# Hybrid decoder block: two heads' q and k as one pair of seven products, and the order of the gate pairs

## The chip, the cores and the metric

The kernel runs on one core of one Trainium2 chip. The metric is the device time of one execution in microseconds. A profile is one execution taken by the hardware profiler; its span runs from the first to the last instruction of the program. In the profile PE is TensorE (matmuls, with PEld its weight loads), DVE is VectorE, ACT is ScalarE, POOL is GpSimd and SP is SyncE, which here only issues transfers.

## The reference

One decoder block on 512 tokens of width 1024, in float32:

```python
hn = rmsnorm(x, g_mix)
(xa, ba, ca, za, q, k, v, o, zb, ig, fg, ga, gb) = split(hn @ w_in)        # w_in: 1024 x 14344
ya = (ba * causal_short_conv(ca * xa, conv_w, conv_b) * silu(za)) @ w_a_out
hb = mlstm_chunkwise(q, k, v, ig + b_i, fg + b_f)                           # 4 heads, dk 256, dv 512
yb = (sigmoid(o) * rmsnorm(hb, g_head) * silu(zb)) @ w_b_out
x = x + (sigmoid(ga) * ya + sigmoid(gb) * yb) @ w_o
x = x + sigmoid(rmsnorm(x, g_ple) @ w_ple_gate) * (p @ w_ple)
return rmsnorm(x, g_final)
```

q and k are 1024 columns each (256 for a head), v, o and zb 2048 each (512 for a head), ga and gb 1024 each. The mLSTM of a head needs the scores q k^T under a mask with running gate terms, and multiplies them by v. The kernel takes each head over all 512 tokens at once.

## The kernel before

**Matmuls in three parts.** Each float32 operand is cut into a high part (rounded to the matmul's format, `hi`) and a low part (the rest, `lo`). `mm3` (L203) issues three matmuls: hi x hi, hi x lo, lo x hi. The cut of a weight takes ScalarE for `whi` (L152) and VectorE for `wlo` (L153); each weight operand of 512 x 512 is cut in two halves of 128 x 1024.

**Plain blocks and pairs.** A plain block (`block_fm`, L267) multiplies all 1024 rows of hn by 512 columns of weights: two operands, 2 x 4 x 4 x 3 = 96 matmuls of 512 columns. A pair (`strassen`, L293) does 1024 columns with seven products instead of eight (Strassen's scheme in Winograd's form): the weights' blocks b11, b21, b12, b22 are added up in the raw buffers, and the left side's combinations of hn are kept cut in `hs` (L255). A pair with tokens on the output's partitions takes 7 x 24 = 168 matmuls of 512 columns; with `fm=True` (features on the partitions, 256 tokens of a half along the columns) it takes 7 x 48 = 336 of 256 columns. The convolution's four pairs are of the second kind, all others in this kernel of the first. The outputs of a pair need 6 sums `c` on VectorE (L325) and 8 copies out of PSUM on ScalarE (`snap`, L321); `c` has 3 buffers.

**Weights.** `chunks` lists the transfers and `operands` (L69 to L120) the order in which the products use them. Four raw buffers (`wraw`) rotate; SyncE's queue loads a chunk as soon as a buffer is free. The sums of a pair are made by adding transfers on GpSimd's queue (L159): they read the other block from memory again and add it to a raw buffer, after that buffer's present content has been cut. Where a pair's third sum has an engine (`third`, `dve`), VectorE makes that sum instead (L157).

**Order.** All engines but SyncE execute in the order in which the code emits. After each quarter or half of a product the code calls `step` (L195): a `tick` cuts one half of the next operand and moves every pending generator (`active`) one `yield` on. So a pair has 14 ticks, a plain block 8. An operand is cut one product ahead of its use, and a transfer that adds to a buffer has two products' time.

**Stages.** PLE product and transposes of x into `hn_hi`, `hn_lo` (`turn_x`, L501; GpSimd adds them back to `hnf`, L506); Q0, the plain block of q and k of head 0, kept in memory (`keep_qk`, L621) after its ScalarE copy (L623); between its second half's two middle banks the 16 gate matmuls `psg` (L708), whose small rows then go through `gate_rows` (L637: scans, logarithms, and 14 small transposes `ptc`, L685 and L687); then the pair GB. Beside GB run `gate_rows` and `left` (L611), which makes `hs` from the four combinations at L606 to L609. Then for each head h: q and k (head 0 loads its raw ones back into `qk_raw`; others run a plain block, Q1 to Q3), the pair VO (v and o, with the head's `scores` in its ticks), the weighted sums (L862), and for even heads the pair ZB for this head and the next. `finish` (L908) transposes a head's result and stores it (`yt_d`) in the ticks of the next stage. After head 3 comes the pair GA, then the convolution's four pairs, the products with w_a_out, w_b_out, w_o and w_ple_gate, and the last norm.

So the order of the large stages is Q0, GB, VO0, ZB0, Q1, VO1, Q2, VO2, ZB2, Q3, VO3, GA, convolution.

Of the kernel before, what the change touches and what calls it, by code (L numbers as in the profile page):

```python
# [14 lines left out]
P = 128  # L15
# [21 lines left out]
def hybrid_block(ctx, tc, x, p, g_mix, w_in, conv_w, conv_b, w_a_out, b_gates, g_head,  # L37
# [206 lines left out]
    qk_d = dram.tile([P, 4, S], F32, name="qk_d")  # L244
# [118 lines left out]
    def sink_conv(c, u, v, ya, ct):  # L363
# [13 lines left out]
        def put(src, h):  # L377
            to = [t[:, c:c + 2, h * H2:(h + 1) * H2] for t in ya]
# [122 lines left out]
    def turn_x(k):  # L501
# [4 lines left out]
        pool.tensor_tensor(hnf[:, k, :], hn_hi[:, k, :].bitcast(F32), hn_lo[:, k, :].bitcast(F32), ALU.add)  # L506
# [95 lines left out]
    a11, a12 = (hnf[:, c * HC:(c + 1) * HC, :H2] for c in range(2))  # L602
    a21, a22 = (hnf[:, c * HC:(c + 1) * HC, H2:] for c in range(2))
    hsf = [sp.tile([P, HC, H2], F32, name=f"hsf{i}", tag=f"hsf{i}", align_bytes=256) for i in range(2)]

    dve.tensor_tensor(hsf[0], a22, a21, ALU.subtract)  # L606
    dve.tensor_tensor(hsf[1], hsf[0], a11, ALU.add)
    dve.tensor_tensor(a12, hsf[1], a12, ALU.subtract)
    dve.tensor_tensor(a21, a11, a21, ALU.subtract)  # L609

    def left():  # L611
        for i, src, scale in ((0, hsf[0], 1.0), (3, a12, 1.0), (1, hsf[1], -1.0), (2, a21, 1.0)):
            act.activation(hs[i][0], src, AF.Copy, scale=scale)
            yield
            dve.scalar_tensor_tensor(hs[i][1], src, scale, hs[i][0].bitcast(F32), ALU.mult, ALU.subtract)
            yield
# [4 lines left out]
    def keep_qk(m, ps):  # L621
        u = temp("eevv"[m], "qk_s")
        act.activation(u, ps, AF.Copy)  # L623
        nc.gpsimd.dma_start(qk_d[:, m, :], u)
        yield
# [11 lines left out]
    def gate_rows():  # L637
# [14 lines left out]
        yield  # L652
# [39 lines left out]
        for _ in range(4):  # L692
            yield
        act.activation(enm.rearrange("p t h -> p (t h)"), colsb[:, 40:], AF.Exp)

    colsb = const.tile([P, 56], F32, name="colsb")
    enm = const.tile([P, NT, NH], F32, name="enm")

    w = next_operand()
    for m in range(4):  # L700
# [3 lines left out]
        step(keep_qk(m, pss[m]))  # L704
        if m == 1:
            psg = ps_x.tile([P, S], F32, name="psg", tag="x")
            for k in range(KT):
                pe.matmul(psg, lhsT=wg[:, k, :], rhs=hn_hi[:, k, :], start=k == 0, stop=False)  # L708
                pe.matmul(psg, lhsT=wg[:, k, :], rhs=hn_lo[:, k, :], start=False, stop=k == KT - 1)
            active.append(gate_rows())  # L710
# [10 lines left out]
    strassen(hn_lhs, sink_gate(0))  # L721
# [27 lines left out]
    def scores(h, qk, pr, pp, done, raw):  # L749

        if raw is not None:
            yield
            yield
            for m in range(4):
                cut(qk[0][:, m, :], qk[1][:, m, :], raw[:, m, :])
                if m == 1:
# [8 lines left out]
                          cmask.unsqueeze(1).broadcast_to([P, NT, P]), ALU.add)  # L765
        sc, e = {}, {}
# [26 lines left out]
    def head(h):  # L793
        qk, vv = [], []

        def cut_qk(m, ps):
            if not qk:
                both = hp.tile([P, 2, 4, S], F32R, name="qk", tag="qk", align_bytes=256)
                qk.extend(both[:, i] for i in range(2))
            if m is None:  # L800
                return
            cut(qk[0][:, m, :], qk[1][:, m, :], ps)
            yield

        raw = None
        if h == 0:
            next(cut_qk(None, None), None)
# [438 lines left out]
```

## Time and profile before

| | |
|---|---|
| median of 3 runs | 871.14 us (869.73 to 873.0) |
| the profiled execution's own time | 871.68 us |
| its span | 869.7 us |
| granted TensorE clock, mean | 0.996 |
| transfers | 169.65 MB, mean 195 GB/s |

Busy times of engines are unions of their instructions' spans. A matmul's recorded duration is longer than the distance to the next one, since matmuls overlap; what one costs is read from the distance of starts. A wait is put down to the instruction that released it. The chain lists, backwards from the last instruction, what each step waited for.

### The profile page before, as it was taken

The page shows a single profiled execution, that of the slowest core. Times are in us where ns is not written, and L with a number is a line of the kernel's source. Part 1 is how long each engine was busy: PE and PEld are TensorE (multiplying, and loading weights), DVE is VectorE, ACT ScalarE, POOL GpSimd, SP SyncE. Part 2 cuts the span into 40 slices and gives each one's busy share as a digit, 9 for nine tenths or more (in the row PEclk, how much of TensorE's full clock was granted, in tenths as well). Part 3 has the DMA queues.
Part 4 walks back from the last instruction along what each step waited for, and adds up shares of the span by engine and source line. Part 5 has one row for each costly group of instructions (what it writes and reads, how often), then busy time and mean ns, then how long its engine had stood idle before and what let it go on. Part 6 is the DMA issues. An engine that isn't in the chain of part 4 may idle for free.

```text
span 869.7 us, 11799 instructions
## 1 busy us (share of the span) xinstructions
PE 852.3 (98%) x4507; PEld 732.3 (84%) x4507; DVE 599.8 (69%) x774; ACT 468.4 (54%) x674; POOL 255.8 (29%) x246
## 2 busy tenths in 40 slices
PE   7999999999999999999999999999999999999995
PEld 6877888888888888888888999999998888788885
DVE  4769676774674666755785588898986777864465
ACT  5575676555563755547656555545453256534342
POOL 3742422322333132331331424333410224030031
PEclk9999999999999999999999999999999999999999
DMA  8799996968855887867869989899898588994002
GB/s 289 262 210 220 275 221 127 223 233 193 177 163 145 191 176 158 238 193 158 236 122 269 230 192 163 202 181 181 181 326 309 97 194 211 272 329 157 1 1 97
DMA packets 100728, 169.65 MB, mean 195 GB/s; under 512 B 6272, under 2 KB 44224, under 8 KB 99392
## 3 DMA queue, kind: packets, MB, share of 16 engines
q0 software_dynamic: 39312, 76.03, 45.1%
q1 hardware_dynamic: 60208, 90.78, 31.5%
q10 hardware_dynamic: 1152, 2.10, 0.7%
q8 instruction: 35, 0.57, 0.3%
q14 instruction: 21, 0.17, 0.1%
HBM read 153.16 MB, written 15.73 MB: 194 GB/s over the span
## 4 chain that ended last, share of the span: by engine, by line
PE 80%; DMA 6%; issue 4%; DVE 4%; ACT 2%; POOL 2%; POOLq 0%; SPq 0%; DVEq 0%; ACTq 0%
PE mm L206 24%; PE mm L207 24%; PE mm L205 24%; DMA wraw<-in_w_in 3%; DMA wraw<-in_w_b_out 2%; DVE wlo L153 2%; PE pv L205 1%; ACT whi L152 1%; PE pv L206 1%; PE pv L207 1%; POOL wraw L159 1%; PE pty L744 1%; DMA sg_d<-c 1%; DMA pin<-in_p 0%; PE sc L207 0%
## 5 line engine op out<-in xcount | busy, mean ns | idle before, releaser
L153 DVE TENSOR_TENSOR wlo<-wraw,whi 128x1024 fp32r<-128x1024 f32 x234 | 299.1, 1281 | 127.3 <-ACT whi L152 127.0
L152 ACT ACTIVATE whi<-wraw 128x1024 fp32r<-128x1024 f32 x236 | 247.0, 1054 | 105.2 <-PE mm L207 44.7
L159 POOL DMA_DIRECT2D wraw<-in_w_in x110 | 136.0, 1402 | 289.1 <-DVE wlo L153 218.5
L205 PE MATMUL mm<-hn_hi,whi 128*128 128x256 f32 (+1 forms) x320 | 105.1, 328 | 0.0
L207 PE MATMUL mm<-hn_hi,wlo 128*128 128x256 f32 (+1 forms) x320 | 104.4, 326 | 0.2 <-POOL wlo L153 0.2
L206 PE MATMUL mm<-hn_lo,whi 128*128 128x256 f32 (+1 forms) x320 | 104.2, 326 | 0.0
L206 PE MATMUL mm<-wlo,hs 128*128 128x512 f32 x256 | 100.7, 393 | 1.1 <-DVE wlo L153 1.0
L205 PE MATMUL mm<-whi,hs 128*128 128x512 f32 x256 | 101.0, 394 | 0.3 <-DVE c L325 0.3
L207 PE MATMUL mm<-whi,hs 128*128 128x512 f32 x256 | 100.2, 391 | 0.0
L321 ACT ACTIVATE s<-mm 128x512 f32<-128x512 f32 x78 | 46.4, 595 | 94.6 <-PE mm L207 94.5
L206 PE MATMUL mm<-wlo,hn_hi 128*128 128x512 f32 x192 | 74.9, 390 | 0.2 <-DVE wlo L153 0.2
L205 PE MATMUL mm<-whi,hn_hi 128*128 128x512 f32 x192 | 75.0, 391 | 0.0
L207 PE MATMUL mm<-whi,hn_lo 128*128 128x512 f32 x192 | 74.8, 389 | 0.0
L207 PE MATMUL mm<-hs,wlo 128*128 128x256 f32 x256 | 72.5, 283 | 0.8 <-DVE wlo L153 0.8
L205 PE MATMUL mm<-hs,whi 128*128 128x256 f32 x256 | 72.5, 283 | 0.0
L206 PE MATMUL mm<-hs,whi 128*128 128x256 f32 x256 | 72.4, 283 | 0.0
L207 PEld LDWEIGHTS mm<-hn_hi,wlo 128*128 128x128 f32 x320 | 60.9, 190 | 5.7 <-POOL wlo L153 0.8
L206 PEld LDWEIGHTS mm<-hn_lo,whi 128*128 128x128 f32 x320 | 60.9, 190 | 4.7
L205 PEld LDWEIGHTS mm<-hn_hi,whi 128*128 128x128 f32 x320 | 60.9, 190 | 4.6
L206 PEld LDWEIGHTS mm<-wlo,hs 128*128 128x128 f32 x256 | 48.5, 190 | 11.9 <-DVE wlo L153 2.4
L205 PEld LDWEIGHTS mm<-whi,hs 128*128 128x128 f32 x256 | 48.5, 189 | 10.8 <-DVE c L325 0.7
L207 PEld LDWEIGHTS mm<-whi,hs 128*128 128x128 f32 x256 | 48.5, 189 | 10.1
(276 smaller groups left out, 1680.0 us busy)
## 6 DMA issues: line engine op xcount, KB each, us to landing
wraw<-in_w_in SPq DMA_DIRECT2D x32, 1024.0 KB, 6.1
wraw<-in_w_in POOLq DMA_DIRECT2D x62, 512.0 KB, 6.8
wraw<-in_w_in SPq DMA_DIRECT2D x48, 512.0 KB, 4.5
wraw<-in_w_in POOLq DMA_DIRECT2D x48, 256.0 KB, 5.8
wraw<-in_w_b_out SPq DMA_DIRECT2D x8, 1024.0 KB, 6.4
wraw<-in_w_b_out POOLq DMA_DIRECT2D x16, 512.0 KB, 7.4
yt_d<-yc POOLq DMA_DIRECT2D x4, 1024.0 KB, 7.6
wraw<-in_w_a_out SPq DMA_DIRECT2D x4, 1024.0 KB, 8.9
```

What stands on the lines that cost most here:

```text
L152: act.activation(hi, t, AF.Copy)
L153: (e_lo or dve).tensor_tensor(lo, t, hi.bitcast(F32), ALU.subtract)
L159: nc.gpsimd.dma_start(raws[to][:, ks, cs], src[:, ks, :], accum_op=ALU.add)
L205: pe.matmul(ps, lhsT=a[0], rhs=b[0], start=first, stop=False, **kw)
L206: pe.matmul(ps, lhsT=a[0], rhs=b[1], start=False, stop=False, **kw)
L207: pe.matmul(ps, lhsT=a[1], rhs=b[0], start=False, stop=last, **kw)
L321: act.activation(to[i], src, AF.Copy, scale=scale)
L744: pe.transpose(pts[v][:, t * P:(t + 1) * P], y[:, t, v * P:(v + 1) * P], ident)
```

## The change

- q and k of head 1 become a second plain block at the front (Q1), straight after Q0, kept in memory as head 0's are. Q2 and Q3 become one pair with `fm=True` and VectorE for the third sum, QK23, at the start of head 2; its first output (head 2) is cut in place, its second (head 3) goes to memory and comes back as `qk_raw`.
- The pair GB moves behind ZB0, inside head 0's turn of the loop; GA moves behind ZB2, ahead of head 3.
- `hnf` is made by ScalarE from PSUM instead of by GpSimd from `hn_hi` and `hn_lo`.
- The gate matmuls `psg` move ahead of Q0's second half, and `gate_rows` starts with its first tick. The four left combinations move into `left`, which now runs in Q1's ticks.
- `scores` always waits two ticks; the exponential `enm` moves from `gate_rows` into head 0's scores; `cols` moves to a lasting pool; the `drain` after GA is gone, and `ya` is made when the convolution first writes it.

The order of the large stages becomes Q0, Q1, VO0, ZB0, GB, VO1, QK23, VO2, ZB2, GA, VO3, convolution.

```diff
     qk_block(0)
-    pair(w_in_v, [(GB, CW)], [(GB + CW, CW)])
+    qk_block(1)
     for h in range(NH):
-        if h > 0:
-            qk_block(h)
         pair(w_in_v, [(V + h * DV, DV)], [(O + h * DV, DV)])
         if h % 2 == 0:
             pair(w_in_v, [(ZB + h * DV, DV)], [(ZB + (h + 1) * DV, DV)])
-    pair(w_in_v, [(GA, CW)], [(GA + CW, CW)], dve)
+            pair(w_in_v, [((GB, GA)[h // 2], CW)], [((GB, GA)[h // 2] + CW, CW)], dve if h else None)
+        elif h == 1:
+            pair(w_in_v, *([(Q + i * DK, DK), (K + i * DK, DK)] for i in (2, 3)), dve)
...
-        pool.tensor_tensor(hnf[:, k, :], hn_hi[:, k, :].bitcast(F32), hn_lo[:, k, :].bitcast(F32), ALU.add)
+        act.activation(hnf[:, k, :], pt, AF.Copy, scale=gm[:, k:k + 1])
...
-    dve.tensor_tensor(hsf[0], a22, a21, ALU.subtract)
-    dve.tensor_tensor(hsf[1], hsf[0], a11, ALU.add)
-    dve.tensor_tensor(a12, hsf[1], a12, ALU.subtract)
-    dve.tensor_tensor(a21, a11, a21, ALU.subtract)
-
     def left():
+        dve.tensor_tensor(hsf[0], a22, a21, ALU.subtract)
+        dve.tensor_tensor(hsf[1], hsf[0], a11, ALU.add)
+        yield
+        dve.tensor_tensor(a12, hsf[1], a12, ALU.subtract)
+        dve.tensor_tensor(a21, a11, a21, ALU.subtract)
+        yield
...
     w = next_operand()
+    psg = ps_x.tile([P, S], F32, name="psg", tag="x")
+    for k in range(KT):
+        pe.matmul(psg, lhsT=wg[:, k, :], rhs=hn_hi[:, k, :], start=k == 0, stop=False)
+        pe.matmul(psg, lhsT=wg[:, k, :], rhs=hn_lo[:, k, :], start=False, stop=k == KT - 1)
+    active.append(gate_rows())
     for m in range(4):
...
-        step(keep_qk(m, pss[m]))
-        if m == 1:
-            psg = ps_x.tile([P, S], F32, name="psg", tag="x")
...
+        step(keep_qk(0)(m, pss[m]))
...
     active.append(left())
-    strassen(hn_lhs, sink_gate(0))
+    block_fm(keep_qk(1))
     drain()
...
+        def sink_qk(n, t, src):
+
+            fs, ps = slice(2 * (t % 2), 2 * (t % 2) + 2), slice(t // 2 * H2, (t // 2 + 1) * H2)
+            src = src.rearrange("p (f s) -> p f s", f=2)
+            if n == 1:
+                nc.gpsimd.dma_start(qk_d[h + 1][:, fs, ps], src)
+                return
...
+            cut(*[u[:, fs, ps] for u in qk], src)
             yield
...
-        if h == 0:
...
+        if h == 2:
+            strassen(hn_lhs, sink_qk, True)
+        else:
+            qk_tile()
             raw = hp.tile([P, 2, 4, S], F32, name="qk_raw", tag="vv", align_bytes=256)[:, 0]
             for m in range(4):
-                nc.sync.dma_start(raw[:, m, :], qk_d[:, m, :])
-        else:
-            block_fm(cut_qk)
+                nc.sync.dma_start(raw[:, m, :], qk_d[h][:, m, :])
...
         active.append(finish(h, y, 2 + h % 2))
-    strassen(hn_lhs, sink_gate(2))
-    drain()
+        if h % 2 == 0:
+            strassen(hn_lhs, sink_gate(h))
     close(hq_ctx)
```

**VectorE at the front.** These are VectorE's instructions from the cut of Q0's second operand on (`wlo20`, `wlo21`: operand 2, halves 0 and 1; `wlo30`: the next operand), with the gate weights `wg` and the left combinations `hsf`, `hnf`. Before:

```order
L153 TENSOR_TENSOR wlo20_417<-wraw2_327,whi20_416 128x1024
L153 TENSOR_TENSOR wlo21_433<-wraw2_327,whi21_432 128x1024
L595 CAST wg_136<-wg_raw_138 128x8x4
L596 TENSOR_TENSOR wg_136<-wg_raw_138,wg_136 128x8x4
L595 CAST wg_136<-wg_raw_138 128x8x4
L596 TENSOR_TENSOR wg_136<-wg_raw_138,wg_136 128x8x4
L599 CAST sel_90<-ident_74 4x512 x2
L606 TENSOR_TENSOR hsf0_444<-hnf_153 128x1024
L607 TENSOR_TENSOR hsf1_445<-hsf0_444,hnf_153 128x1024
L608 TENSOR_TENSOR hnf_153<-hsf1_445,hnf_153 128x4x256
L609 TENSOR_TENSOR hnf_153<-hnf_153 128x4x256
```

After:

```order
L153 TENSOR_TENSOR wlo21_437<-wraw2_329,whi21_436 128x1024
L597 CAST wg_138<-wg_raw_140 128x8x4
L598 TENSOR_TENSOR wg_138<-wg_raw_140,wg_138 128x8x4
L597 CAST wg_138<-wg_raw_140 128x8x4
L598 TENSOR_TENSOR wg_138<-wg_raw_140,wg_138 128x8x4
L601 CAST sel_90<-ident_74 4x512 x2
L153 TENSOR_TENSOR wlo30_483<-wraw3_332,whi30_482 128x1024
L153 TENSOR_TENSOR wlo31_504<-wraw3_332,whi31_503 128x1024
L649 TENSOR_TENSOR rows_448<-rows_448,psg_453 4x512 x2
L655 TENSOR_SCALAR rows_448<-rows_448 4x512
L656 SCALAR_TENSOR_TENSOR rows_448<-rows_448 4x512
L153 TENSOR_TENSOR wlo40_562<-wraw4_335,whi40_561 128x1024
```

The gate weights keep their place behind the cut of operand 2; the left combinations are gone from here, and the gate rows come sooner.

**TensorE at the small transposes.** `ptc` transposes the gate `rows`; `hs20`, `hs21` are the cut left side of GB's sixth product, `whi81` its operand, `wlo41` that of Q1's second half, `wlo50` belongs to the first operand of VO0. Before, in the middle of GB's sixth product:

```order
L206 MATMUL mm_542<-wlo81_772,hs20_118 128x512
L207 MATMUL mm_542<-whi81_771,hs21_119 128x512
L685 MATMUL ptc_799<-ident_74,rows_450 128x4 x10
L687 MATMUL ptc_799<-ident_74,rows_450 128x4 x4
L205 MATMUL mm_566<-whi80_747,hs20_118 128x512
L206 MATMUL mm_566<-wlo80_748,hs20_118 128x512
```

After:

```order
L207 MATMUL mm_613<-hn_hi_109,wlo41_584 128x512
L691 MATMUL ptc_715<-ident_74,rows_448 128x4 x10
L693 MATMUL ptc_715<-ident_74,rows_448 128x4 x4
L205 MATMUL mm_752<-whi50_644,hn_hi_109 128x512
L206 MATMUL mm_752<-wlo50_645,hn_hi_109 128x512
```

The transposes now stand at the border between Q1 and VO0.

**GpSimd's queue at VO3.** `wraw33` and `wraw35` (before) and `wraw37` and `wraw39` (after) are b11 and b12 of the pair, `pp` the running sums of the scores, `gty` the tile of head 3's output gates, loaded from `z_d3`. Before:

```order
L159 DMA wraw35_3096<-in_w_in 128x2x512 x2
L159 DMA wraw33_3000<-in_w_in 128x2x512 x2
L788 TENSOR_TENSOR pp_3263<-pp_3263 128x384
L159 DMA wraw33_3000<-in_w_in 128x2x512
L838 DMA gty_3467<-z_d3_103 128x2048
L788 TENSOR_TENSOR pp_3263<-pp_3263 128x256
```

After:

```order
L159 DMA wraw39_3681<-in_w_in 128x2x512 x2
L159 DMA wraw37_3494<-in_w_in 128x2x512 x4
L793 TENSOR_TENSOR pp_3782<-pp_3782 128x384
L850 DMA gty_4054<-z_d3_105 128x2048
L793 TENSOR_TENSOR pp_3782<-pp_3782 128x256
L793 TENSOR_TENSOR pp_3782<-pp_3782 128x128
```

The load of `gty` moved behind all adding transfers of the pair.

More of the change, by code (lines that the diff above doesn't have):

```diff
@@ L243, in hybrid_block @@
     yt_d = [dram.tile([P, 2, HC, H2], F32, name=f"yt_d{h}") for h in range(NH)]
-    qk_d = dram.tile([P, 4, S], F32, name="qk_d")
+    qk_d = {h: dram.tile([P, 4, S], F32, name=f"qk_d{h}") for h in (0, 1, 3)}
     sg_d = [dram.tile([P, NT, CW], F32, name=f"sg_d{g}") for g in range(4)]
@@ L377, in put @@
         def put(src, h):
+            if not ya:
+                ya.extend(hp.tile([P, KT, S], F32R, name=f"ya{i}", tag=t, align_bytes=256) for i, t in enumerate(("qk", "vv")))
             to = [t[:, c:c + 2, h * H2:(h + 1) * H2] for t in ya]
```

54 lines of the change are left out of this document (25 added, 29 removed).

## The prediction

> **What bounds the kernel now.** I read the page's busy times first, then TensorE's waits, then the timeline for the spacing of matmuls.
>
> ```profile
> PE 852.3 (98%) x4507; PEld 732.3 (84%) x4507; DVE 599.8 (69%) x774; ACT 468.4 (54%) x674; POOL 255.8 (29%) x246
> ```
>
> ```profile
> PE ptp L485 <- DMA pin<-in_p: 5.1, 2, 3.6
> PE mm L206 <- DVE wlo L153: 1.9, 3, 1.0
> PE mm L207 <- DVE wlo L153: 0.8, 1, 0.8
> ```
>
> TensorE is busy for 98% of the span, and its waits on other engines (total, times, longest) are few. So the time is the sum of TensorE's instructions by their spacing, plus a handful of lost microseconds. The spacing comes from TensorE's timeline, first and last row of two even stretches: 168 steps with 256 columns, then 168 steps with 512.
>
> ```profile
> 539.76 0.28 PE L205 MATMUL mm<-hs,whi 128*128 128x256 f32 x1
> ...
> 559.92 0.28 PE L205 MATMUL mm<-hn_hi,whi 128*128 128x256 f32 x1
> ```
>
> ```profile
> 661.90 0.39 PE L205 MATMUL mm<-whi,ya 128*128 128x512 f32 x1
> ...
> 699.99 0.39 PE L205 MATMUL mm<-whi,l 128*128 128x512 f32 x1
> ```
>
> 20.16 us / 168 = 0.1200 us for 256 columns; 38.09 us / 168 = 0.2267 us for 512. The 0.28 and 0.39 in the rows are durations that overlap; only the spacing counts.
>
> The lost time has one large place, the gate pair GB, which now runs straight after q and k of head 0 (Q0). Here are its first matmul, and the mask product L759 that follows the first 48 matmuls of head 0's v and o pair (VO0):
>
> ```profile
> 50.31 0.39 PE L205 MATMUL mm<-whi,hn_hi 128*128 128x512 f32 x1
> ...
> 104.78 0.50 PE L759 MATMUL pnb<-nmr,sel 64*128 64x512 f32 x1
> ```
>
> Between them stand 168 + 48 matmuls of 0.2267, 49.0 us, and 14 small transposes (0.96 us, the two ptc rows below), together 49.9; the rows are 54.5 apart. So about 4.5 us are lost there. The chain of waits shows how:
>
> ```profile
> 76.27 1.19 DVE hs L615
> ...
> 80.44 1.15 DVE wlo L153
> ...
> 81.63 0.50 PE mm L206
> ...
> 83.06 0.71 PE ptc L685 x10
> 83.77 0.25 PE ptc L687 x4
> 84.03 0.72 PE mm L205
> 84.75 0.43 PE mm L206
> ...
> 86.88 0.43 PE mm L205
> ```
>
> The chain runs through VectorE, a queue of weight splits (wlo), gate rows and left operands (hs), and TensorE waits for a split. After the small transposes the matmuls stand 0.43 apart instead of 0.23, up to 87.3: the clock was halved, about 7 x 0.2 = 1.4 of the 4.5 us.
>
> **The products.** Two plain blocks (Q2, Q3), 2 x 96 = 192 matmuls of 512 columns, go; one pair of seven products with 256 columns (QK23), 7 x 48 = 336, comes. -192 x 0.2267 + 336 x 0.1200 = -43.5 + 40.3 = **-3.2 us**, all of it on the path, since TensorE is the path. The Trainium skill ("TensorE: Matmul & The Clock Gate", Back-to-back issue gap) gives an isolated spacing of columns / 2.4 GHz + 2.5 ns, 109 and 216 ns; by it the term would be -4.7. The rows say 120 and 227, and they decide.
>
> **What GB leaves behind.** After the change plain Q1 follows Q0, and GB runs behind head 0, when the gate rows and left operands are long done. The 4.5 us go: **-4.5**. What is late next? First the gate matmuls psg (L708): they move ahead of the second half of Q0 and need wg from VectorE. The front's rows, from the timeline (Q0's second half starts with the last one):
>
> ```profile
> 20.74 1.84 ACT L215 ACTIVATE hn_hi<-pt,prm 128x512 fp32r<-128x512 f32 x3
> ...
> 26.85 0.69 ACT L215 ACTIVATE hn_hi<-pt,prm 128x512 fp32r<-128x512 f32 x1 [1.13 <-PE pt L504]
> ...
> 30.58 7.01 POOL L506 TENSOR_TENSOR hnf<-hn_hi,hn_lo 128x512 f32<-128x512 f32 x4
> 31.09 2.95 ACT L152 ACTIVATE whi<-wraw 128x1024 fp32r<-128x1024 f32 x3
> ...
> 34.13 2.31 DVE L153 TENSOR_TENSOR wlo<-wraw,whi 128x1024 fp32r<-128x1024 f32 x1
> ...
> 35.81 0.39 PE L205 MATMUL mm<-hn_hi,whi 128*128 128x512 f32 x1
> ```
>
> ```profile
> 36.36 1.26 DVE L595 CAST wg<-wg_raw 128x32 fp32r<-128x32 f32 x1
> ...
> 37.77 0.17 DVE L595 CAST wg<-wg_raw 128x32 fp32r<-128x32 f32 x1
> 37.98 0.19 DVE L596 TENSOR_TENSOR wg<-wg_raw,wg 128x32 fp32r<-128x32 f32 x1
> ...
> 58.96 1.21 DVE L153 TENSOR_TENSOR wlo<-wraw,whi 128x1024 fp32r<-128x1024 f32 x1
> ```
>
> Today wg is done at 37.98 + 0.19 = 38.2. Two things shift it. ScalarE makes hnf now: 8 copies of 1.84 / 3 = 0.61, +4.9 us in a queue whose idle gaps (three like the 1.13 above) take 3.4, so the splits of operand 2 start 1.5 later, near 32.6. And GpSimd's additions are gone, beside which VectorE's split took 2.31 and its first cast 1.26, against 1.21 and 0.17 otherwise. Operand 2's two splits then end near 32.6 + 1.0 + 2 x 1.21 = 36.0, and wg four small steps (0.7) later, 36.7. psg wants to start at 35.81, so it waits 0.9; 0 if ScalarE packs tighter, 1.4 if operand 2 is another half microsecond late. I take **+0.5**. The first half of Q0 needs slices 0 to 3 of hn alone, and these are earlier in ScalarE's queue.
>
> Second, the 14 transposes ptc. They now stand between Q1 and VO0 and need the last gate rows. VectorE's work on two tiles (length, then TensorE, weight loads, VectorE, ScalarE; tile rows first, then hs):
>
> ```profile
> 45.00:90.00 45.00, 1.03 (x14) 0.95 (x14) 12.08 (x29) 3.25 (x5) 0.96 0.92 222
> ...
> 45.00:90.00 45.00, 25.01 (x96) 18.80 (x96) 4.82 (x4) 4.17 (x4) 0.96 0.92 222
> ```
>
> With four combinations of the left side (operands as large as a split's, 4 x 1.21 = 4.8) and six splits (7.3) that is 12.1 + 4.8 + 4.8 + 7.3 = 29.0 us. TensorE has 16 psg + 48 (Q0) + 96 (Q1) matmuls there, 160 x 0.2267 = 36.3, so the work fits. But it is not spread. ScalarE's copy of Q0's last bank (at 36.3 + 64 x 0.2267 = 50.8) stands ahead of the split of operand 4, so VectorE idles until 50.8 + 0.6 + 1.0 = 52.4. From there to the last row that ptc needs stand four splits (4.8), the four combinations (4.8), three hs (3.6) and 23 of the 29 steps on rows, some 8.5 us (9.6 by the mean, but the six left out are long ones): 21.7 us, ready at 74.1. TensorE arrives at 36.3 + 36.3 + 0.7 (ten transposes) = 73.3. It waits 0.8, or nothing if the steps overlap as they do in the chain above (a split each 1.15), or 2.0 if another split slips ahead: **+0.6**. The clock may halve again after these transposes, as it did at 84, between 0 and 1.4: **+0.5**. The Trainium skill (same page, Why this matters for your kernels) has the clock fall only after idle gaps of over some 3 us; by it this term is 0. The rows show the halved clock after a wait of 1 us and the small transposes, so I keep the upper bound.
>
> **Transfers.** Two smaller losses stand in the chain, at VO3 and from the pair GA into the convolution's first pair:
>
> ```profile
> 418.31 10.20 DMA wraw<-in_w_in
> ...
> 430.91 0.50 PE mm L206
> ```
>
> ```profile
> 473.88 6.08 DMA sg_d<-c
> 480.06 0.41 DVE c L325
> ...
> 482.18 2.19 POOL wraw L159 x2
> 484.37 9.13 DMA wraw<-in_w_in
> ...
> 495.98 0.39 PE mm L207
> ```
>
> At 430.9 an adding transfer (L159) took 10.20 us beside the 1 MB load of z_d; of the 1.9 us that L206 waited, 1.0 is at 81, so about 0.4 is here. After the change that load is issued later, behind the pair's adding transfers: **-0.4**, at worst 0. At 496.0 the wait is the 0.8 of L207. After the change GA is followed by VO3, whose adding transfers are one issue a half instead of two (half of 2.19 sooner); and between VO3 and the convolution stand the weighted sums, 30 matmuls or 6.8 us in which no operand is used up: **-0.8**, at worst 0. For junctions that no row shows (the weighted sums into QK23, GA into VO3) I add **+0.5**: each between 0 and the 0.8 of that row.
>
> Nothing is charged for the rest. The raw q and k of heads 1 and 3 come back as head 0's do today; scores start up to three steps later and still end three steps before the weighted sums. Four late multiplications and small steps of head 3 move under the convolution's first pair:
>
> ```profile
> 496.00:536.00 40.00, 40.00 (x333) 40.00 (x334) 33.18 (x46) 20.66 (x26) 14.68 (x12) 1.00 0.92 185
> ```
>
> VectorE is busy 33.2 of 40 there; four steps on half a split's elements, at most 1.21 each, make it 38. If that cover fails, the price is 1 to 2 us.
>
> **The sum.** -3.2 - 4.5 + 0.5 + 0.6 + 0.5 - 0.4 - 0.8 + 0.5 = -6.8. The profiled execution took 871.68, so 864.9; the median of the three runs, 871.14, lies 0.5 lower, so 864.4.
>
> **The rivals.** *VectorE's queue comes along.* The gate rows and left operands have 160 matmuls of cover instead of 16 + 48 + 168 = 232, and the queue, not the order, was the cause: TensorE waits 1.0 at psg and 2.5 at ptc and VO0's second operand, with the halved clock (1.4). For it: TensorE's wait at 81 has VectorE's queue before it. Against: GB's own work on VectorE (its operands and sums) leaves that stretch. Time: -3.2 - 4.5 + 4.9 - 1.2 + 0.5 = -3.5, so 867.6 (866.8 to 870.5): no change by the bound below.
>
> *The adding transfers fall behind: slower.* ZB0, GB, VO1 and ZB2, GA, VO3 now follow one another without plain blocks, and those blocks gave the queues room.
>
> ```profile
> 190.00:212.00 22.00, 22.00 (x105) 17.99 (x104) 8.15 (x9) 11.15 (x15) 5.51 (x5) 1.00 0.84 191
> 212.00:250.00 38.00, 38.00 (x176) 31.70 (x175) 26.76 (x30) 25.91 (x43) 13.75 (x12) 1.00 0.76 194
> ```
>
> The share before the last number is that of the 16 DMA engines: 0.84 in Q1, 0.76 in VO1, 0.92 in the convolution above. The rival decides when an adding transfer takes over about 9 us, since those of 9.13 and 10.20 cost 0.8 and 0.4. Three fed operands a pair, five pairs (GB, VO1, QK23, VO2, VO3), 0.8 each: +12, so 876. Against it: GB and VO0 stand back to back today, and the convolution's pairs run on at 0.1200.
>
> **How the numbers follow.** Forecast 0.66; the queue 0.25; the transfers 0.09. A measurement can tell about 0.5%, 4.4 us, from no change: faster means under 866.8. The forecast's own bounds are 861.5 (no new wait, 1.6 + 0.5 less, and a little more) to 866.8; the range goes on to 870.5 for the first rival and leaves the second out. So faster 0.66, same 0.25, slower 0.09.
>
> **What would show it.** Right: spacing 0.120 in the rows of QK23, no wait over 0.9 at psg, Q1 ending near 73, full clock from VO0 on, waits of TensorE of about 2 us beside the load of p. Wrong: a wait at psg over 1.5 us or at ptc over 2, releases by wlo at VO0's second operand, or waits on wlo in GB, VO1, QK23 whose chain leads to DMA wraw.

## The result, and the profile after

The changed kernel takes **885.17 us** (median of 4 runs, 881.07 to 885.75), the kernel before in the same session 870.56 (median of 4, 869.73 to 873.0). The ratio is 1.0165, 95% interval 1.014 to 1.019: **slower by 1.65%**. The forecast was 864.4 with a range from 861.5 to 870.5; the rival that ends slower had been given 0.09 and priced at 876. The profiled execution took 885.75 us, its span is 884.0, the mean clock 0.991.

The page's first row, and TensorE's waits on other engines (in total, times, longest):

```profile
PE 852.7 (96%) x4651; PEld 737.6 (83%) x4651; DVE 615.6 (70%) x788; ACT 484.2 (55%) x699; POOL 263.1 (30%) x258
```

```profile
PE psg L706 <- DVE wg L598: 4.7, 1, 4.7
PE mm L206 <- DVE wlo L153: 4.6, 8, 0.8
...
PE mm L205 <- DVE c L325: 2.8, 2, 1.7
PE mm L205 <- ACT whi L152: 2.0, 2, 1.0
...
PE mm L207 <- POOL wlo L153: 1.8, 2, 1.6
```

TensorE is as busy as before in microseconds, but its share fell from 98 to 96%: it waits. One wait of 4.7 us stands at the gate matmuls, and one of 1.6 in Q0's first half (its wlo, made by GpSimd, comes late too); the others are spread. The busy time of engines by stretches, with the clock, the share of the 16 DMA engines and the GB/s as last three columns (the columns before them are PE, PEld, DVE, ACT, POOL), for QK23, GB, GA and VO3 in this order:

```profile
272.00:312.00 40.00, 40.00 (x337) 40.00 (x336) 28.34 (x35) 23.53 (x33) 14.95 (x14) 1.00 0.79 198
184.00:223.00 39.00, 37.24 (x172) 30.50 (x170) 18.99 (x20) 23.57 (x32) 13.39 (x17) 1.00 1.06 287
401.00:440.00 39.00, 38.16 (x175) 31.14 (x174) 26.52 (x26) 23.17 (x31) 9.53 (x9) 1.00 0.96 245
440.00:480.00 40.00, 38.85 (x177) 31.98 (x177) 27.80 (x33) 29.41 (x47) 13.97 (x13) 1.00 1.06 267
```

QK23's 336 matmuls run at 40.00 / 337 = 0.119 without a gap: the pair itself does what it says. In GB, GA and VO3 TensorE has gaps, and the DMA engines are full (shares of 0.96 to 1.06).

Where the time is lost can be added up from TensorE's timeline: the distance of each matmul's start to the next, less the even spacing of its shape (0.2267 us for 512 columns, 0.1200 for 256). By stretches of the span, for the two kernels and for the experiments that matter most below:

| lost on TensorE, us | 0-20 | 20-60 | 60-110 | 110-380 | 380-520 | 520-end | sum | span |
|---|---|---|---|---|---|---|---|---|
| before | 5.2 | 0.7 | 4.7 | 1.2 | 2.0 | 1.8 | 15.6 | 869.7 |
| changed | 4.9 | 11.0 | 3.5 | 6.1 | 3.1 | 4.3 | 32.9 | 884.0 |
| hnf_before_lo | 4.0 | 1.1 | 3.3 | 6.2 | 4.9 | 1.7 | 21.3 | 872.2 |
| few_gate_stores | 3.6 | 1.4 | 3.2 | 3.9 | 2.5 | 2.2 | 16.7 | 867.6 |
| reload_early | 3.5 | 2.0 | 5.3 | 3.8 | 1.8 | 4.0 | 20.4 | 871.3 |
| cuts_later | 5.1 | 1.1 | 1.2 | 3.1 | 1.9 | 4.6 | 17.0 | 868.1 |
| loop_only | 3.6 | 1.3 | 3.1 | 1.2 | 5.9 | 2.5 | 17.7 | 868.6 |
| reload_early_loop | 4.8 | 1.3 | 3.1 | 1.5 | 1.8 | 2.0 | 14.6 | 865.3 |

Span less loss is 854.1 before and 851.1 after: the products' gain of 3 us is there, and 17.3 us of new loss lie over it. The first and last columns differ from run to run of one kernel too (loading, and the last products), so they are not read further. Each row is one profiled execution: that of loop_only took 870.39 us (the slowest of ten, median 868.63), of reload_early 873.11 (the slowest of twelve, median 871.17), of cuts_later 869.93 (the slowest of five, median 866.98). So a row tells where time is lost, and the medians and ratios tell how much a version takes.

The largest item is at 20 to 60 us. The chain of waits there (start, length, what):

```profile
20.59 0.70 ACT hn_hi L215
...
21.31 0.76 DVE hn_lo L216
...
22.09 0.69 ACT hnf L508
22.78 0.59 ACT hn_hi L215
...
23.39 0.76 DVE hn_lo L216
...
24.18 0.69 ACT hnf L508
...
37.21 0.59 ACT hn_hi L215
...
37.83 0.76 DVE hn_lo L216
...
39.20 1.05 ACT whi L152
...
40.28 2.36 DVE wlo L153 x2
```

The chain goes from ScalarE to VectorE and back for every slice of x: hn_hi, then hn_lo, then hnf, then the next hn_hi, 2.09 us a slice (from hnf at 22.09 to hnf at 24.18). In the built program the copy to hnf waits for VectorE's hn_lo of the same slice, though both only read the PSUM tile pt. So ScalarE's queue isn't packed with copies; it waits in each slice for VectorE. ScalarE's timeline shows it at the row's end (idle before, and who ended it):

```profile
22.09 0.69 ACT L508 ACTIVATE hnf<-pt,prm 128x512 f32<-128x512 f32 x1 [0.82 <-DVE hn_lo L216]
```

The splits of operand 2 come out at 39.2 to 42.6, wg behind them, and psg at 43.42 instead of the 36 or so of the forecast. After that wait the clock is halved:

```profile
43.42 0.76 PE L706 MATMUL psg<-hn_hi,wg 128*128 128x512 f32 x1 [4.69 <-DVE wg L598]
...
44.41 0.63 PE L706 MATMUL psg<-hn_hi,wg 128*128 128x512 f32 x1
44.83 0.63 PE L707 MATMUL psg<-hn_lo,wg 128*128 128x512 f32 x1
```

The starts are 0.43 apart instead of 0.23. Of the 11.0 us lost there, the wait and these slow starts make up some 7.5 and the wait in Q0's first half 1.8.

### The profile page after: what moved, and what is told of

It reads as the page before. It is cut to its first block, busy times and chain, and to the rows that moved or that the text cites. A ratio compares the mean times of both kernels' runs of the same rounds, so it can differ in the third digit from the quotient of the medians.

```text
span 884.0 us, 12211 instructions
## 1 busy us (share of the span) xinstructions
PE 852.7 (96%) x4651; PEld 737.6 (83%) x4651; DVE 615.6 (70%) x788; ACT 484.2 (55%) x699; POOL 263.1 (30%) x258
## 4 chain that ended last, share of the span: by engine, by line
PE 73%; DMA 10%; DVE 7%; ACT 4%; issue 3%; POOL 1%; SPq 0%; POOLq 0%; ACTq 0%; DVEq 0%
PE mm L206 22%; PE mm L207 22%; PE mm L205 22%; DMA wraw<-in_w_in 6%; DVE wlo L153 3%; DMA wraw<-in_w_b_out 2%; ACT whi L152 2%; DMA qk_raw<-qk_d 1%; PE pv L205 1%; PE pv L206 1%; PE pv L207 1%; DVE hn_lo L216 1%; POOL wraw L159 1%; PE pty L747 1%; DMA pin<-in_p 1%
## 5 line engine op out<-in xcount | busy, mean ns | idle before, releaser
L153 DVE TENSOR_TENSOR wlo<-wraw,whi 128x1024 fp32r<-128x1024 f32 x240 | 308.3, 1288 | 142.8 <-ACT whi L152 142.2
L152 ACT ACTIVATE whi<-wraw 128x1024 fp32r<-128x1024 f32 x242 | 253.0, 1053 | 112.2 <-PE mm L207 42.4
L159 POOL DMA_DIRECT2D wraw<-in_w_in x122 | 151.5, 1423 | 277.7 <-DVE wlo L153 179.3
L207 PE MATMUL mm<-hn_hi,wlo 128*128 128x256 f32 (+1 forms) x304 | 93.1, 306 | 1.8 <-POOL wlo L153 1.8
L205 PE MATMUL mm<-hn_hi,whi 128*128 128x256 f32 (+1 forms) x304 | 93.3, 307 | 0.3 <-ACT ple L515 0.3
L206 PE MATMUL mm<-hn_lo,whi 128*128 128x256 f32 (+1 forms) x304 | 93.0, 306 | 0.3 <-DVE hn_lo L216 0.3
L205 PE MATMUL mm<-hs,whi 128*128 128x256 f32 x320 | 90.9, 284 | 0.0
L206 PE MATMUL mm<-hs,whi 128*128 128x256 f32 x320 | 90.5, 283 | 0.0
L207 PE MATMUL mm<-hs,wlo 128*128 128x256 f32 x320 | 90.5, 283 | 0.0
L206 PEld LDWEIGHTS mm<-hs,whi 128*128 128x128 f32 x320 | 61.4, 192 | 0.0
L205 PEld LDWEIGHTS mm<-hs,whi 128*128 128x128 f32 x320 | 61.4, 192 | 0.0
L207 PEld LDWEIGHTS mm<-hs,wlo 128*128 128x128 f32 x320 | 61.4, 192 | 0.0
```

Source lines behind the costliest of these rows:

```text
L152: act.activation(hi, t, AF.Copy)
L153: (e_lo or dve).tensor_tensor(lo, t, hi.bitcast(F32), ALU.subtract)
L159: nc.gpsimd.dma_start(raws[to][:, ks, cs], src[:, ks, :], accum_op=ALU.add)
L205: pe.matmul(ps, lhsT=a[0], rhs=b[0], start=first, stop=False, **kw)
L206: pe.matmul(ps, lhsT=a[0], rhs=b[1], start=False, stop=False, **kw)
L207: pe.matmul(ps, lhsT=a[1], rhs=b[0], start=False, stop=last, **kw)
```

## The experiments

The versions are compared by the ratio of their time to that of the kernel before, run beside them on the same chip. Two theories stood at the start. **A (front):** the new place of the hnf copy chains ScalarE and VectorE, and nothing else is wrong in the front; its rival **W** says that ScalarE simply has too much work there. **B (loop):** where pairs follow one another the transfers come too late, because there are too many of them; this was the second rival of the prediction. **C** came later: one certain transfer, the reload of raw q and k, is late and stands in the way.

### The front: who makes hnf, and in which order

**hnf_on_gpsimd**: the changed kernel with hnf made by GpSimd again.

```diff
-        act.activation(hnf[:, k, :], pt, AF.Copy, scale=gm[:, k:k + 1])
+        pool.tensor_tensor(hnf[:, k, :], hn_hi[:, k, :].bitcast(F32), hn_lo[:, k, :].bitcast(F32), ALU.add)
```

> The changed kernel with one line undone: hnf is made by GpSimd from hn_hi and hn_lo again. Theory A (in the changed kernel ScalarE's copy hnf waits for VectorE's hn_lo of the same slice, so each slice takes 2.1 us in a chain ScalarE-VectorE-ScalarE, and psg waits 4.7 us for wg): the chain goes, VectorE's splits beside GpSimd's additions cost 2.3 us each again, psg waits about 2.4 us; the lost time between 20 and 60 us falls from 11.0 to about 3; 877 us. Rival L (the order of the pairs in the loop costs everything): 883 us or more.

Measured: 880.52 us, ratio 1.0114 (1.0077 to 1.0152). The wait at psg fell from 4.7 to 2.7, and was followed by the halved clock again. So the front of the changed kernel has no room for GpSimd's slow additions either, and the gain, 4.7 us (885.17 to 880.52), is little more than half of the 8 that theory A had hoped for.

**hnf_before_lo**: the same work on the same engines, only ScalarE's copy to hnf ahead of VectorE's hn_lo.

```diff
-        cut(hn_hi[:, k, :], hn_lo[:, k, :], pt, gm[:, k:k + 1])
-        act.activation(hnf[:, k, :], pt, AF.Copy, scale=gm[:, k:k + 1])
+        g = gm[:, k:k + 1]
+        act.activation(hn_hi[:, k, :], pt, AF.Copy, scale=g)
+        act.activation(hnf[:, k, :], pt, AF.Copy, scale=g)
+        dve.scalar_tensor_tensor(hn_lo[:, k, :], pt, g, hn_hi[:, k, :].bitcast(F32), ALU.mult, ALU.subtract)
```

> The changed kernel with the order inside turn_x changed: ScalarE makes hn_hi and then hnf, and only then VectorE's hn_lo is issued. ScalarE does exactly the work of the changed kernel. Theory A: hnf no longer waits, ScalarE packs its copies, psg waits under 1 us; 875 to 876 us. Rival W (ScalarE's added work of 4.9 us is the cause, not the wait): within 2 us of the changed kernel, 883 to 885. Rival L: 883 or more.

Measured: 875.22 us, ratio 1.0059 (1.0034 to 1.0084). The loss at 20 to 60 us fell from 11.0 to 1.1. ScalarE's timeline in the same place:

```profile
20.77 0.69 ACT L508 ACTIVATE hn_hi<-pt,prm 128x512 fp32r<-128x512 f32 x1
21.35 0.70 ACT L509 ACTIVATE hnf<-pt,prm 128x512 f32<-128x512 f32 x1
21.91 0.70 ACT L508 ACTIVATE hn_hi<-pt,prm 128x512 fp32r<-128x512 f32 x1
```

A slice now takes 1.14 us of ScalarE (20.77 to 21.91) instead of 2.09, with no wait in it. Theory A is shown; W falls, since ScalarE has exactly the same work.

**only_hnf**: the kernel before with the one line, hnf copied by ScalarE behind hn_lo.

> The kernel before with one line of the change alone: hnf made by ScalarE behind hn_lo. Theory A: the splits of Q0's second operand end near 42 instead of 36, Q0's second half waits 5 to 6 us, and VectorE's queue for GB starts as late; 877 to 881 us. Rival L or W with the 3.4 us of ScalarE's idle time as cover: 871 to 873.

Measured: 878.72 us, ratio 1.0083 (1.0057 to 1.0108). The line costs the kernel before some 7 us as well, by the ratio, without any other part of the change. (The profiled execution is the fastest of nine, 873.11; even it loses 6.7 us at 20 to 60.)

### The loop: transfers, or one transfer

**loop_only**: the front as before (Q0, GB, VO0, ZB0), Q1 as a plain block behind it, then the new pair QK23 and GA behind ZB2.

```diff
     qk_block(0)
+    pair(w_in_v, [(GB, CW)], [(GB + CW, CW)])
-    qk_block(1)
     for h in range(NH):
+        if h == 1:
+            qk_block(1)
...
-            pair(w_in_v, [((GB, GA)[h // 2], CW)], [((GB, GA)[h // 2] + CW, CW)], dve if h else None)
+            if h:
+                pair(w_in_v, [(GA, CW)], [(GA + CW, CW)], dve)
```

> The kernel before with its front untouched (GB behind Q0, gate rows beside it) and of the loop only this part of the change: q and k of heads 2 and 3 as a pair (QK23), GA behind ZB2. Q1 stays a plain block between ZB0 and VO1. Theory B (the transfers fall behind where GB stands between ZB0 and VO1): no such stretch here, the products give -3.2, GA into the convolution -0.8; 867 to 869 us. Rival P (the pair QK23 and GA's new place cost by themselves): 872 or more.

Measured: 868.63 us, ratio 0.9986 (0.9969 to 1.0003). The products' gain arrives only in part: the trace loses 4.7 us between GA and VO3 (in the column 380-520, 5.9 against 2.0 before). There the chain shows one adding transfer:

```profile
408.00 14.03 DMA wraw<-in_w_in
...
423.14 1.24 DVE wlo L156
```

14 us, where an adding transfer of 512 KB has a median of 7.8 in this kernel's list of issues.

**thirds_changed**, **thirds_loop_only**, **thirds_before**: if there are too many adding transfers, fewer help. Every pair of w_in makes its third sum on VectorE, which takes two of eight adding transfers (one sum of four, each in two halves) from the pairs that had none there: in hnf_before_lo, in loop_only, and as a control in the kernel before.

```diff
-    def pair(view, p1, p2, third=None):
+    def pair(view, p1, p2, third=dve):
```

> The kernel of hnf_before_lo (875.2), with VectorE making the third sum of every pair on w_in, as GA and the convolution do: one of four adding transfers of a pair goes, VectorE gets two additions of 128 x 1024 more a pair (2.4 us). Theory B (what the loop lost, about 9 us from 160 to 450 us in the trace, is adding transfers of 10 to 14 us where GB and GA stand between other pairs): half or more of it comes back, 870 to 872 us. Rival V (VectorE and GpSimd hold each other up there): no gain, 875 or more.

> The kernel of loop_only (868.6) with the third sums on VectorE. Theory B: the 4.7 us lost at GA into VO3 (waits of 1.0, 1.0 and a halved clock) mostly go; GB at the front loses up to 2 us more, since VectorE's queue bounds it; 865 to 867 us. Rival V: 868 to 871.

> The kernel before (870.0) with the third sums on VectorE, as a control. Theory B: its plain blocks leave the transfers room, so there is little to win (0.4 at VO3), and GB at the front, bound by VectorE's queue, loses 1 to 2.5: 870 to 873 us. If the third sums help by themselves wherever they are: 868 or less.

Measured: 874.86 us, ratio 1.0047 (1.002 to 1.0074); 874.31, ratio 1.0066 (1.004 to 1.0092); 875.54, ratio 1.0083 (1.0064 to 1.0101). The first comes out at its rival's 875, the other two above both their ranges. The first gains next to nothing over 1.0059 (its profiled execution loses some 13 us from 110 to 520, that of hnf_before_lo 11.1), the two with GB in the front lose some 6 us. VectorE's queue in the control shows why: a sum of 1.21 (L157) stands among the gate rows (L659) and splits that TensorE needs at GB,

```profile
68.72 1.21 DVE L153 TENSOR_TENSOR wlo<-wraw,whi 128x1024 fp32r<-128x1024 f32 x1
69.85 1.21 DVE L157 TENSOR_TENSOR wraw<-wraw,wraw 128x1024 f32<-128x1024 f32 x1
70.99 1.35 DVE L659 TENSOR_TENSOR_SCAN rows<-ones,rows 4x128 f32<-4x128 f32 x4
```

and TensorE waits 2.6 us for wlo between 55 and 110. So the number of adding transfers is not what costs, or VectorE's price eats up the gain; these runs alone can't tell the two apart.

**few_gate_stores**: the other traffic in these stretches is what the gate pairs store. hnf_before_lo with a quarter of the gates' stores: of each gate half only the first of four token blocks is stored, and the later loads read this block four times. So 3 MB of 4 MB of stores are left out, and no load is.

```diff
-            (nc.scalar if g else nc.gpsimd).dma_start(sg_d[g + n][:, t, :], sg)
+            if t == 0:
+                (nc.scalar if g else nc.gpsimd).dma_start(sg_d[g + n][:, t, :], sg)
```

> The kernel of hnf_before_lo (875.2) that stores only the first of four token blocks of each gate half and loads that block for all four: 3 MB of the gates' 4 MB of stores are left out, and the gates of the other blocks are wrong. Theory B in the form that the gates' stores are the surplus that makes the adding transfers late: the waits behind GB and GA shrink, 871 to 873 us. If the adding transfers of pairs back to back are late by themselves: 874 to 876.

Measured: 870.64 us, ratio 1.0011 (0.9992 to 1.0029), against 1.0059 with all stores. The loss from 110 to 520 falls from 11.1 to 6.4 us. Transfers do meet here, then: taking 3 MB out helps by 4.6 us (875.22 to 870.64). But GA's stores ran into the convolution in the kernel before and cost 1.1 us there, which suggests that something else fills the queues as well.

### The reload of raw q and k

SyncE's waits in the changed kernel name it. L824 is the reload of q and k into qk_raw:

```profile
SPq L824 <- DMA yt_d<-yc: 22.7, 2, 15.3
```

The buffer of qk_raw (the tag vv) also serves `yc`, the transposed result of the head before. So the reloads of heads 1 and 3 start only when that result is stored, about the middle of GB and GA (at 202 and 424 us), with SyncE's queue (the weights) behind them. Then 1 MB in four pieces goes out beside the gates' stores and the adding transfers for the next products. In the kernel before only head 0 has such a reload; it too stands where two pairs meet, at the end of GB (issued at 85.5 to 87.7 us, landed in 4.9 to 7.6), but no head's result is stored beside it, and hardly a loss follows. The chain of the changed kernel at the reload in GB begins with an adding transfer of 10.73 us:

```profile
200.78 10.73 DMA wraw<-in_w_in
211.53 1.06 ACT whi L152
212.62 1.24 DVE wlo L153
```

The reload's own row among the DMA issues (KB each, median us to landing):

```profile
qk_raw<-qk_d SPq DMA_DIRECT2D x12, 256.0 KB, 9.1
```

The next four versions put these reloads elsewhere. The two halves of `pr`, the cut scores, are free from a head's weighted sums on; the raw q and k of the next head fit there (2 x 4 KB of 2 x 5 KB a partition). The code emits the load in the sixth tick of ZB0 or ZB2, and SyncE's queue, which runs ahead, issues it at their start (127.9 and 351.6 us in reload_early). Head 0's raw q and k go into `pr` too, at their old place in the order.

```diff
+    def load_qk(h, wait):
+        for _ in range(wait):
+            yield
+        prs[h] = [hq2.tile([P, 1280], F32R, name=f"pr{i}", align_bytes=256) for i in range(2)]
+        for m in range(4):
+            nc.sync.dma_start(prs[h][m // 2][:, m % 2 * S:m % 2 * S + S].bitcast(F32), qk_d[h][:, m, :])
...
-            raw = hp.tile([P, 2, 4, S], F32, name="qk_raw", tag="vv", align_bytes=256)[:, 0]
...
         active.append(rsqrt())
+        if h % 2 == 0:
+            active.append(load_qk(h + 1, 5))
```

**reload_early** is hnf_before_lo with this.

> The same work as in the version with hnf ahead of hn_lo (875.2 us). There the reload of raw q and k of heads 1 and 3 (1 MB each) writes a buffer of the tag vv, so it can start only once the result of the head before it (yt_d) has been stored: SyncE's queue stood 24.7 us in two such waits, and the reload's median was 8.7 us, in the stretch in which the next pair's adding transfers run. Here the reload goes into the two buffers pr of the scores, which are free from the weighted sums on, and starts in the sixth tick of ZB0 and ZB2. Theory C (the reload, held by yt_d and landing among the adding transfers, makes the losses behind GB and GA: 2.3 + 0.7 + 1.2 us at 200 to 243 us, 0.7 + 3.9 at 391 to 446): some 7 of these 8.8 go, 868 (866 to 870). Theory B (the sum of the transfers is too large there, wherever the reload stands, since none is left out): 873 to 875.

Measured: 871.17 us, ratio 1.0018 (0.9999 to 1.0036). No store of yt_d holds SyncE's queue any more, and the pieces land in less than half the time (a median over head 0's pieces as well; those of heads 1 and 3 whose landing the traces show took 8.7 and 6.0 us in hnf_before_lo and 3.2 to 4.1 here):

```profile
pr<-qk_d SPq DMA_DIRECT2D x12, 256.0 KB, 4.1
```

The queue itself stands at these two reloads as long as before, 24.7 us in hnf_before_lo and 23.8 here, only earlier, until the weighted sums have read `pr`:

```profile
SPq L807 <- PE pv L207: 23.8, 2, 11.9
```

So what helps is not a freer queue but the hour of the reload. In hnf_before_lo the DMA engines' share is 1.08 from 191 to 203 us, where it lands in GB; in reload_early it is 0.69 from 127.5 to 135, in ZB0.

TensorE's waits between 195 and 260 us, first of hnf_before_lo,

```profile
PE mm L206 <- DVE wlo L153: 1.9, 3, 0.9
PE mm L205 <- ACT whi L152: 1.1, 1, 1.1
```

and then of reload_early:

```profile
PE mm L206 <- DVE wlo L153: 0.8, 1, 0.8
PE mm L205 <- ACT s L321: 0.5, 1, 0.5
```

The losses from 110 to 520 fell from 11.1 to 5.6 us, where theory C had wanted some 7 less. The time fell by 4.1 us (875.22 to 871.17) and lies between the ranges of the two theories. The profiled execution loses 5.3 at 60 to 110 (below), against 3.3 in hnf_before_lo; whether head 0's reload into `pr` does that or this execution alone was not followed.

**reload_early_loop** is loop_only with head 3's reload moved in the same way.

> The version with the front as before and only the loop changed (868.6 us), with head 3's raw q and k loaded into the buffers pr during ZB2 instead of into vv behind the store of yt_d. By theory C the 4.7 us that its trace lost between GA and VO3 (at 420 to 428 us) go: 864.5 (863 to 866), faster than before by more than a half per cent, which is the forecast of the products' 3.3 us with a part of the junctions' waits. By theory B 867.5 to 869.

Measured: 867.07 us, ratio 0.9973 (0.9957 to 0.9988). The loss at 380 to 520 fell from 5.9 to 1.8: nothing was left out, one load stands elsewhere. This version beats the kernel before; the expected 863 to 866 was too low by 1. The medians are only 1.6 us apart (868.63 and 867.07) and the intervals of the two ratios overlap, so the trace shows the loss gone, and this time alone would not decide between C and B, which wanted 867.5 to 869.

**reload_early_ga_last** and **reload_early_q1_front_ga_last** put GA behind VO3 again, in the two versions.

> As the version before it in this list, and the pair GA stands behind VO3 again, ahead of the convolution, as in the kernel before; only QK23, Q1's place and the early reload are left of the change. If a gate pair between ZB2 and VO3 costs time by itself (its 2 MB of stores and its adding transfers among those of the neighbours): 863 to 864 and below the version with GA behind ZB2 by 1 us or more. If only the late reload did, the two are within 0.7 us of each other. If VO3 straight behind ZB2 is worse than with GA between (yt_d, z_d and the gate loads meet): 867 or more.

> The version with hnf ahead of hn_lo and the early reload, with GA behind VO3 again; GB stays behind ZB0. With the run before it in this list it makes a square of two fronts (GB or Q1 after Q0) by two places of GA. By theory C it is like the first of this list, 868 (866 to 870); if gate pairs inside the loop cost by themselves, 866 to 867. The front of the change (Q1 in GB's place) was to gain some 4 us: then it stands 2 to 4 us below the version with the front as before; if it comes out above it, GB's move is the part that gains nothing.

Measured: 873.51 us, ratio 1.0047 (1.003 to 1.0065), and 877.35, ratio 1.0093 (1.007 to 1.0116): 0.74% and 0.75% slower than with GA behind ZB2. Of the first expectation the third case came true; the second version came out above both of its ranges. With VO3 straight behind ZB2, head 2's result is still being stored from the buffer that head 3's v needs. The chain of the first:

```profile
396.14 10.80 DMA wraw<-in_w_in
406.94 5.71 DMA yt_d<-yc
...
412.67 0.63 ACT vv L853
413.30 0.49 ACT v L323
```

A pair of gates between two heads is thus no burden; it gives the turn of the result its time. Theory B, that the sum of the transfers is too large wherever the reload stands, falls for most of the new loss by reload_early, which leaves none out; of the 5.6 us that still go from 110 to 520, 2.4 more than before, no run shows the cause.

The four versions also answer for the front. With the new front (Q1 behind Q0, GB behind ZB0) the kernel takes 4 us more than with GB in its old place (871.17 against 867.07, and 877.35 against 873.51): up to here GB's move gains nothing.

**cuts_later**: what was left at 60 to 110 is head 0's reload. Its wait on SyncE's queue, in the kernel before and in the changed kernel:

```profile
SPq L810 <- DVE nmr L689: 3.4, 1, 3.4
```

```profile
SPq L824 <- DVE nmr L695: 18.3, 1, 18.3
```

The heads' buffers take the place of the front's, and the reload is released by nmr, one of the gate rows' last steps. Before, it was issued at 85.5 us, and the end of GB and the first ticks of VO0 lay between it and its first cut at 101.0; now VO0 begins at once, the reload is issued at 85.9, and the first cut stands at 92.8. In reload_early ScalarE stands at the four cuts, with the copies out of PSUM behind them:

```profile
83.26 0.63 ACT L212 ACTIVATE qk<-pr 128x512 fp32r<-128x512 f32 x1 [2.87 <-DMA pr<-qk_d]
85.28 0.63 ACT L212 ACTIVATE qk<-pr 128x512 fp32r<-128x512 f32 x1 [1.40 <-DMA pr<-qk_d]
```

TensorE's longest wait there, between 60 and 110 us, is for a sum `c` of the pair:

```profile
PE mm L205 <- DVE c L325: 2.7, 1, 2.7
```

The version cuts head 0's raw q and k two ticks later, in one tick.

```diff
         if raw is not None:
+            for _ in range(2 if h == 0 else 0):
+                yield
             for m in range(4):
                 cut(qk[0][:, m, :], qk[1][:, m, :], raw[m])
-                if m == 1:
+                if m == 1 and h:
                     yield
```

> The version with hnf ahead of hn_lo and the early reload of heads 1 and 3 (871.2 us), in which head 0's four cuts of raw q and k stand in one tick two ticks later. There the reload of head 0 left SyncE's queue at 75.3 us, when VectorE's nmr had freed the start's space, landed piece by piece at 83.3, 85.3, 86.8 and 88.6, and ScalarE stood at these pieces' cuts at 82 to 88.6 with the next weights' whi and the copies out of PSUM behind them: 2.8 us of waits and 1.6 us of half clock in its trace. If that reload holds the front of the changed kernel back: 867 (866 to 868.5), below the kernel before by 0.2 to 0.4%. If the cuts only move the wait (the scores end a tick later, and the first half of gt comes later): 870 to 872.

Measured: 866.98 us, ratio **0.9957** (0.9943 to 0.9971). Between 60 and 110 us that wait is gone, and this is the one row left:

```profile
PE ptc L695 <- DVE rows L688: 0.2, 1, 0.2
```

So the change in full, with three things mended (the order of two reads of pt, the place of two reloads, the tick of four cuts), is faster than the kernel before, by 0.43%. That is less than the half per cent from which the prediction meant to speak of a change, but the interval leaves 1 out.

## Why the prediction was wrong, point by point

Three steps lead from the changed kernel to one that is faster than before, each with its own cause: ratio 1.0165 as given, 1.0059 with hnf ahead of hn_lo, 1.0018 with the early reloads, 0.9957 with head 0's cuts later. In medians: 885.17, 875.22, 871.17, 866.98. The forecast was 864.4; of the 20.8 us above it these steps take away 18.2. Two of the prediction's own signs of being wrong appeared: a wait over 1.5 us at psg, and waits on wlo in GB and VO1 whose chain leads to DMA wraw.

- **The products, -3.2: right.** Spacing 0.119 in QK23, and span less loss is 3.0 lower.
- **psg and wg, +0.5: the step that failed worst.** It reads "8 copies of 1.84 / 3 = 0.61, +4.9 us in a queue whose idle gaps (three like the 1.13 above) take 3.4". That adds up ScalarE's work and takes its gaps as free. But the copy to hnf waits for hn_lo, on another engine, so each slice became a chain of three, 2.09 us instead of 1.14. The term was some 10 us (885.17 to 875.22) with the halved clock in it. The Trainium skill ("PSUM — Partial Sum Buffer", PSUM bank collisions raise a hardware error) has a rule for this: ScalarE and VectorE must not touch one PSUM bank at once, reads against reads included, and a compiler's scheduler puts a dependency between two such instructions. The trace agrees: 0.82 us of idle ScalarE ahead of each hnf, ended by hn_lo. That this rule is why the program has the wait is not shown by a run. The prediction counted hnf's reads of pt as free of the other engine's. Had the copy packed as the step assumed, the step would have held: in hnf_before_lo psg starts at 35.0, without a wait over 0.2.
- **"The raw q and k of heads 1 and 3 come back as head 0's do today": failed, charged at nothing.** They don't: head 0's reload waited 3.4 us for its space, theirs 22.7 for a result on its way out of the buffer, and so they landed in GB and GA among full DMA engines. The price is some 4 us (875.22 to 871.17). The prediction listed the moved blocks and not the moved load, nor what else is under way when its buffer comes free.
- **GB's loss at the front, -4.5: came in part.** The place lost 4.7 before and 3.5 in the changed kernel, because head 0's reload, which the end of GB had covered, now stood bare; 1.2 in cuts_later. The prediction asked what is late next and named psg and ptc, not this reload; its price is some 4 us (871.17 to 866.98), of which the rows at 60 to 110 show 2.3 against the changed kernel (3.5 to 1.2). Even then little is gained in the whole: cuts_later and reload_early_loop differ in GB's place above all, and their ratios, 0.9957 (0.9943 to 0.9971) and 0.9973 (0.9957 to 0.9988), overlap. By the table 1.9 us are gained at 60 to 110 and 1.6 given back at 110 to 380.
- **ptc, +0.6, and the clock after it, +0.5:** the wait was 0.2, and the clock stayed full there. The Trainium skill's rule ("TensorE: Matmul & The Clock Gate", Why this matters for your kernels), by which this term was 0, held at this place, though a wait of 0.2 hardly tests it. It did not hold at the end (below).
- **VO3, -0.4, and the junctions, +0.5: wrong sign and size.** In hnf_before_lo the stretches 110-380 and 380-520 lose 11.1 us against 3.2 before.
- **GA into the convolution, -0.8: right.** Before, 1.1 us are lost at 494.7 to 496.0; in the changed kernel the timeline shows next to none (0.1) between 460 and 740.
- **The rival "VectorE's queue" (0.25):** fell, ptc waited 0.2. **The rival "adding transfers" (0.09)** had the sign and the symptom right: adding transfers of 10.7 us (14.0 in loop_only), over its limit of 9, and waits on wlo in GB and VO1 and on c in VO3 whose chains lead to DMA wraw. Its cause, the missing plain blocks, was not the main one: with the pairs in the same order and the reload elsewhere half of the loss from 110 to 520 went. That it got only 0.09 rested on "GB and VO0 stand back to back today"; head 0's reload stands between them, but no head's result is on its way out there.

What stays open: whether the gates' stores still cost anything once the reloads are early (few_gate_stores and reload_early were not combined). In few_gate_stores the reload landed no faster (median 9.2 us) and the loss shrank all the same, so it seems to be the meeting of the transfers that costs; which of them have to move is not settled. What changes the table's last column from run to run was not followed.

## What to carry to other kernels

A copy that is moved to another engine has to be priced with the wait that the built program gives it, not with its length: place it ahead of the other engine's use of the same tile, and the copies pack. When a block moves, follow the loads that its neighbours covered: ask for each reload which buffer it writes, who had that buffer last, and which other transfers are under way when that buffer comes free. And a block that looks as if it only took transfers may be the time in which a buffer is emptied.

## What the runs showed of the hardware

A wait of 4.7 us at psg was followed by matmuls 0.43 apart; the window 40 to 50 us has a mean clock of 0.66. But much shorter waits can halve it too. TensorE's timeline of the changed kernel near the end:

```profile
763.48 0.49 PE L205 MATMUL mm<-whi,l 128*128 128x512 f32 x1 [1.01 <-ACT whi L152]
764.74 0.50 PE L206 MATMUL mm<-wlo,l 128*128 128x512 f32 x1 [0.77 <-DVE wlo L153]
...
765.54 0.62 PE L206 MATMUL mm<-wlo,l 128*128 128x512 f32 x1
765.96 0.63 PE L207 MATMUL mm<-whi,l 128*128 128x512 f32 x1
```

After two waits of 1.01 and 0.77 us with one matmul between, the starts are 0.42 apart, and the mean clock of the window 760 to 770 us is 0.83. The rule in the Trainium skill ("TensorE: Matmul & The Clock Gate", Why this matters for your kernels: idle time of some 3 us) does not give this. The timeline loses 2.2 us in these two waits and 1.8 by the slow matmuls behind them.

A piece of 256 KB of the reload of heads 1 and 3 took 8.7 us in GB (at a DMA share of 1.08) and 6.0 in GA in hnf_before_lo, and 3.2 to 4.1 in ZB0 and ZB2 in reload_early (at 0.69 in ZB0): the size is the same, only the time of its issue differs.
